# Strassen's seven-product block form for the products with x, in an inference step of a hybrid decoder

## The chip, the cores and the metric

The kernel runs on one core of a Trainium2 chip. The metric is the device time of one execution in microseconds (us). The core has a matrix engine (TensorE, PE in the profile; PEld is its weight load), three engines for elementwise work (VectorE or DVE, ScalarE or ACT, GpSimd or POOL) and SyncE (SP), from whose queue most DMAs are issued. The engines work side by side and wait for each other by semaphores. SBUF is the on-chip memory; PSUM, with banks of 512 fp32 columns, takes TensorE's results. GpSimd is not used on PSUM here.

## What is computed

One step of a decoder with two layers, fp32 in and out, for 1024 prompt tokens and 8 single new tokens (1032 tokens together, model width 1024):

```
# layer 0: gated short convolution          # layer 1: differential attention, 8 heads
b, c, h = split(x @ w_in, 3)                kv = x @ w_kv;  q = rope(x @ w_q)
y = (b * conv3(c * h)) @ w_out              y = rms_norm(softmax(q0 k0) v - lam * softmax(q1 k1) v) @ w_o
# both layers
x = layer_norm(alpha * x + y)
x = layer_norm(alpha * x + (silu(x @ w_gate) * (x @ w_up)) @ w_down)      # inner width 2816
```

The 8 new tokens attend to 256 cached positions each, gathered by a page table, and to themselves (below: decode). Outputs are x after layer 1, the new keys and values, and the last inputs of the convolution.

## The kernel before

All activations lie transposed: 128 features on the partitions, tokens along the columns. The tokens are cut into 3 chunks of 344 columns (CH). Every product has to be exact to nearly fp32, so both operands are split into two fp32r parts, a rounded one and the residual: x into xhf and xlf, a weight tile into whi and wlo. `dense` (L243) makes three matmuls for each of the K tiles: whi by the rounded x (L248), whi by the residual of x (L249), wlo by the rounded x (L251).

A weight tile is 128 x 1024 (8 K tiles by 128 outputs, or as many numbers in another cut). `Stream` (L101) loads it on SP's queue (L112), ACT rounds it to whi (L122) and POOL subtracts to get wlo (L123); 6 pairs are kept ahead. There are 196 such tiles: 24 for w_in, 8 for w_out, 8 each for Q, K, V and w_o, 88 for gate and up of both layers together, 44 for w_down. Where a pass covers one chunk alone, its tiles are loaded and split again for the next chunk.

The program is a list of blocks (L212), each with its weight tiles and its operations. Between the operations `Side` (L141) takes steps of generators that run beside: the layer norms, the first splits of x, the decode. `need` (L256) finishes the norm of a chunk before its first use. Tile, the framework, orders the instructions of each engine and adds the semaphores.

- `conv_mixer` (L423): for each of 8 feature tiles three products c, h, b and the convolution; then w_out, in two halves of K; the second half runs chunk by chunk.
- `ffn` (L384): groups of four (once two) inner tiles; gate and up for the three chunks, silu times up (L398), split into hh and hl (L262, L263), then the down products of the group, added to the residual stream (L359). The first group has its chunks in separate blocks, the last runs chunk by chunk.
- `layer_norm` (L266): sums of the chunk by a matmul with ones, subtraction, squares on ACT, their sum on DVE (L280), reciprocal root, scaling (L305), and the split of the normed x (L300, L302).
- Q and K (`qk_op`, L535) are written to DRAM in their parts. V (`v_steps`, L570) has x as the stationary operand, so that it comes out with tokens on the partitions: products of 128 tokens by 256 columns. Half of V (two of four pairs, EARLY, L184) is made with Q and K.
- `decode` (L617) runs beside K and V: gathers by POOL's queue (L653), products and sums on DVE (L675 to L732).
- `attention` (L770): per head and row block of 128 scores for two maps, exponentials, their difference, transposes, product with V. The other half of V fills it: pieces of `v_steps` are put between the score products. At its end the first products with w_o begin (`begin_project`, L960).
- `project` (L967), the feed-forward of layer 1, and `last_norm` (L318) for the last chunk.

```python
for k in range(nk):
    h, l = xs(k)
    T.matmul(ps, lhsT=hi[:, k, n0:n0 + nn], rhs=h, start=(k == 0), stop=False)
    T.matmul(ps, lhsT=hi[:, k, n0:n0 + nn], rhs=l, start=False, stop=False)
for k in range(nk):
    T.matmul(ps, lhsT=lo[:, k, n0:n0 + nn], rhs=xs(k)[0], start=False, stop=(k == nk - 1))
```

## Time and profile before

| | |
|---|---|
| Time, median of 3 runs | 2614.7 us (2613.64 to 2619.28) |
| The profiled execution | 2612.27 us, its span 2610.5 us |
| TensorE busy | 2495.7 us, 15818 matmuls |
| DVE, ACT, POOL busy | 1299.2, 846.8, 990.6 us |
| Mean granted TensorE clock | 0.982 |

The span goes from the first to the last instruction; little lies around it. Matmuls overlap in the profile (one is shown with some 325 ns, and yet one begins every 157 ns), so their price is read from how many begin in a stretch, not from the duration of one. The duration of an operation on DVE or POOL includes what it waits inside its engine. "x637" behind a busy time is the number of instructions.

### The profile page before, as it was taken

The numbers are of one execution on the slowest core, as the hardware profiler recorded it, in microseconds if no ns is written. First come the engines' busy times: TensorE is split into PE (matmuls) and PEld (weight loads), VectorE is DVE, ScalarE is ACT, GpSimd is POOL, SyncE is SP. The second block draws the span as 40 slices with busy tenths as digits, with TensorE's granted clock in tenths as the row PEclk, the third lists the DMA queues.
The fourth block names the chain that finished last, engine by engine and source line by source line (L and its number), as shares of the span: only waits on it lengthen the run. The fifth ranks groups of instructions, "written<-read, shape, count | busy, mean of one in ns | idle before, by whom it ended". The sixth has DMA issues, their size and how long they took to land. (4 is left out here: it accounts for less than half of the span.)

```text
span 2610.5 us, 38657 instructions
## 1 busy us (share of the span) xinstructions
PE 2495.7 (96%) x15818; PEld 2442.3 (94%) x15818; DVE 1299.2 (50%) x1980; ACT 846.8 (32%) x1534; POOL 990.6 (38%) x545
## 2 busy tenths in 40 slices
PE   8999989999999999989999999898999999999996
PEld 8999889999999999978997899798899999999995
DVE  6335897213222222788387477859723222222277
ACT  3213444211212121443332477734421111111243
POOL 5226555221212223545467243454541222212463
PEclk9999999999999999999999999999999999999998
DMA  4114333111111112336698667543321111111241
GB/s 166 49 49 138 107 116 111 65 41 49 49 49 49 49 42 77 116 127 227 192 328 304 189 181 207 156 164 104 113 97 41 49 49 49 41 48 51 89 152 67
DMA packets 109217, 283.72 MB, mean 109 GB/s; under 512 B 12872, under 2 KB 41960, under 8 KB 108144
## 3 DMA queue, kind: packets, MB, share of 16 engines
q1 hardware_dynamic: 101968, 254.28, 29.8%
q0 software_dynamic: 4608, 16.78, 1.7%
q10 hardware_dynamic: 2464, 10.20, 1.1%
q8 instruction: 124, 2.03, 0.3%
q14 instruction: 53, 0.43, 0.1%
HBM read 242.04 MB, written 39.17 MB: 108 GB/s over the span
## 5 line engine op out<-in xcount | busy, mean ns | idle before, releaser
L123 POOL TENSOR_TENSOR wlo<-wst,whi 128x1024 fp32r<-128x1024 f32 x336 | 832.6, 2484 | 1343.2 <-PE mm L251 662.7
L248 PE MATMUL mm<-xhf,whi 128*128 128x344 f32 x3264 | 1047.6, 325 | 15.7 <-DVE rb L359 7.8
L249 PE MATMUL mm<-xlf,whi 128*128 128x344 f32 x3264 | 1042.0, 323 | 1.8 <-DVE xlf L263 1.8
L248 PEld LDWEIGHTS mm<-xhf,whi 128*128 128x128 f32 x3264 | 622.2, 191 | 19.8 <-DVE rb L359 8.4
L249 PEld LDWEIGHTS mm<-xlf,whi 128*128 128x128 f32 x3264 | 621.7, 190 | 5.2 <-DVE xlf L263 2.5
L122 ACT CAST whi<-wst 128x1024 fp32r<-128x1024 f32 x336 | 351.8, 1049 | 838.3 <-PE mm L249 666.2
L251 PE MATMUL mm<-xhf,wlo 128*128 128x344 f32 x3264 | 587.6, 322 | 0.6 <-POOL wlo L123 0.6
L251 PEld LDWEIGHTS mm<-xhf,wlo 128*128 128x128 f32 x3264 | 533.0, 189 | 1.7 <-POOL wlo L123 0.9
L398 DVE TENSOR_TENSOR t<-mm,t 128x344 f32<-128x344 f32 x132 | 67.8, 514 | 570.4 <-PE mm L251 567.6
L249 PE MATMUL mm<-hl,whi 128*128 128x344 f32 x1056 | 335.3, 323 | 9.2 <-DVE hl L263 9.2
L248 PE MATMUL mm<-hh,whi 128*128 128x344 f32 x1056 | 331.0, 323 | 2.9 <-ACT hh L262 2.0
L251 PE MATMUL mm<-hh,wlo 128*128 128x344 f32 x1056 | 213.5, 320 | 0.0
L249 PEld LDWEIGHTS mm<-hl,whi 128*128 128x128 f32 x1056 | 199.5, 189 | 10.6 <-DVE hl L263 10.6
L248 PEld LDWEIGHTS mm<-hh,whi 128*128 128x128 f32 x1056 | 199.3, 190 | 4.2 <-ACT hh L262 2.6
L359 DVE TENSOR_TENSOR rf<-mm,rf 128x344 f32<-128x344 f32 x192 | 98.2, 514 | 181.4 <-PE mm L251 181.1
L359 DVE TENSOR_TENSOR rb<-mm,rb 128x344 f32<-128x344 f32 x168 | 86.2, 515 | 184.6 <-PE mm L251 184.5
L251 PEld LDWEIGHTS mm<-hh,wlo 128*128 128x128 f32 x1056 | 175.6, 188 | 0.0
L263 DVE TENSOR_TENSOR hl<-t,hh 128x344 fp32r<-128x344 f32 x132 | 144.4, 1096 | 62.0 <-ACT hh L262 61.7
L392 ACT ACTIVATE t<-mm 128x344 f32<-128x344 f32 x132 | 60.0, 457 | 284.3 <-PE mm L251 283.9
L262 ACT CAST hh<-t 128x344 fp32r<-128x344 f32 x132 | 62.9, 479 | 217.9 <-DVE t L398 217.8
L822 DVE CUSTOM_DVE_ANT_0 p<-S,mw 128x256 f32<-128x256 f32 (+7 forms) x128 | 94.4, 753 | 47.1 <-PE S L816 24.3
L824 ACT ACTIVATE p<-p,nm 128x256 f32<-128x256 f32 (+7 forms) x128 | 99.0, 774 | 34.0 <-DVE nm L822 33.5
(194 smaller groups left out, 2382.2 us busy)
## 6 DMA issues: line engine op xcount, KB each, us to landing
wst<-in_wts SPq DMA_DIRECT2D x336, 512.0 KB
qh<-qh SPq DMA_DIRECT2D x64, 128.0 KB
ql<-ql SPq DMA_DIRECT2D x64, 128.0 KB
rf<-in_xT SPq DMA_DIRECT2D x12, 344.0 KB
stash<-rf SPq DMA_DIRECT2D x3, 1376.0 KB
qh<-hi SPq DMA_DIRECT2D x24, 172.0 KB
ql<-lo SPq DMA_DIRECT2D x24, 172.0 KB
out_k<-t SPq DMA_DIRECT2D x24, 172.0 KB
```

Of the source, the lines that this page charges most:

```text
L122: self.nc.scalar.copy(out=hi, in_=st)
L123: self.nc.gpsimd.tensor_tensor(out=lo, in0=st, in1=hi.bitcast(F32), op=ALU.subtract)
L248: T.matmul(ps, lhsT=hi[:, k, n0:n0 + nn], rhs=h, start=(k == 0), stop=False)
L249: T.matmul(ps, lhsT=hi[:, k, n0:n0 + nn], rhs=l, start=False, stop=False)
L251: T.matmul(ps, lhsT=lo[:, k, n0:n0 + nn], rhs=xs(k)[0], start=False, stop=(k == nk - 1))
L262: A.copy(out=hi, in_=src)
L263: V.tensor_tensor(out=lo, in0=src, in1=hi.bitcast(F32), op=ALU.subtract)
L359: V.tensor_tensor(out=R[:, n], in0=ps, in1=R[:, n], op=ALU.add)
L392: A.activation(out=hid[f, c], in_=ps, func=AF.Silu)
L398: V.tensor_tensor(out=sg, in0=ps, in1=sg, op=ALU.mult)
L822: V.tensor_tensor_reduce(out=p[:, 0:n], in0=s[:, 0:n], in1=mw[:, SEQ - n:SEQ], scale=1.0, scalar=1e30, op0=ALU.add, op1=ALU.min, accum_out=nm)
L824: A.activation(out=p[:, 0:n], in_=p[:, 0:n], func=AF.Exp, bias=nm, scale=-1.0, accum_out=l)
```

## The change

The tokens are cut into two chunks of 516, each with half of the prompt and of the new tokens, and each chunk into two halves of 258 columns. A product of two weight tiles (256 outputs), 1024 inputs and 516 tokens is seen as 2 x 2 blocks: outputs by tile, K by halves of 512, tokens by halves of 258. Winograd's variant of Strassen's form makes the four output blocks from 7 block products instead of 8:

- `Stream._prepare` forms the seven weight operands of a pair of tiles: three blocks as they are and four sums, the sums on POOL; each is split by ACT and POOL. Weights now come as half tiles of 128 x 512 (raw, 5 buffers); 4 split operands are kept ahead.
- `blocks_of` and `sums_of` form the seven x operands of a chunk: B11, B21 and B22 as they are and four sums T1 to T4, the sums on POOL; all are split by ACT and DVE. They are made at the start and in every layer norm whose result is multiplied.
- `wino` makes the seven products, some of which add up in PSUM, and joins them on DVE; a `Sink` says what becomes of the four output blocks.

This form is used for w_in, Q, K, V, gate and up, the products with the normed x. The products with w_out, w_o and w_down stay in the old form (`exact`), with 258 columns. Feed-forward groups have two inner tiles (11 groups); the first and the last run chunk by chunk. V is made like K, with features on the partitions, transposed by TensorE and stored, all of it ahead of the attention. The attention has no filling any more; its Q and K tiles lie in the places of x, and its output goes straight to the operand of w_o. The stash of the residual stream moves: chunk 0 is stored before Q, and its place is used for the rotary table and for temporaries; decode has 3 buffers for gathers of K instead of 6. The convolution's result takes the place of x in SBUF, so that w_out's sum reads x from DRAM again. The last norm is no longer shared with POOL. The core of the diff:

```diff
+B11, B21, B22, T1, T2, T3, T4 = range(7)
+NS = 7
+
+WINO = [("A", B11, True), ("B", T2, True), ("A", B21, False), ("B", T3, False), ("C", T1, True), ("E", T4, True),
+        ("C", B22, False)]
...
+    def _prepare(self):
+        task = self.done
+        kind, base = self.tasks[task]
+        self._load(task)
+        nc, g = self.nc, self.nc.gpsimd
+
+        def total(a, b, op):
+            t = self.pool.tile([P, 512], F32, tag="ws", name="ws", bufs=self.sums)
+            g.tensor_tensor(out=t, in0=a, in1=b, op=op)
+            return t
+
+        if kind is None:
+            src = self.raw[base]
+        else:
+            a11, a21, a22, a12 = (self.raw[base + i] for i in range(4))
+            if kind == 1:
+                self.s[1] = total(a21, a22, ALU.add)
+                self.s[2] = total(self.s[1], a11, ALU.subtract)
+            elif kind == 3:
+                self.s[3] = total(a11, a21, ALU.subtract)
+            elif kind == 6:
+                self.s[4] = total(a12, self.s[2], ALU.subtract)
+            src = {0: a11, 2: a12, 5: a22, 1: self.s.get(2), 3: self.s.get(3), 4: self.s.get(1), 6: self.s.get(4)}[kind]
+        hi = self.pool.tile([P, 512], F32R, tag="whi", name="whi", bufs=self.ring)
+        lo = self.pool.tile([P, 512], F32R, tag="wlo", name="wlo", bufs=self.ring)
+        nc.scalar.copy(out=hi, in_=src)
+        g.tensor_tensor(out=lo, in0=src, in1=hi.bitcast(F32), op=ALU.subtract)
         self.ready.append((hi, lo))
-        self.split += 1
+        self.done += 1
...
+        while self.done < min(len(self.tasks), self.taken + self.ring):
...
-    WB, SB = 6, 3
-    RATE = 3
-    PIECES = 4
-    RATE0 = 8
+    RATE = 2
     LAG = 2
-    BEGIN = 4
...
+    xh = [xpool.tile([P, NS, KP, CH], F32R, name=f"xh{p}") for p in range(NP)]
+    xl = [xpool.tile([P, NS, KP, CH], F32R, name=f"xl{p}") for p in range(NP)]
+
+    zh, zl = ([x[p][:, T1:].rearrange("p s k n -> p (s k n)").rearrange("p (k n) -> p k n", k=KT) for p in range(NP)]
+              for x in (xh, xl))
     scr = {n: dram.tile([D, NTOK], F32, name=n) for n in ("qh", "ql", "kh", "kl")}
...
+    def exact(ps, terms, first=True, last=True, **kw):
+
+        for i, ((wh, _), (h, l)) in enumerate(terms):
+            T.matmul(ps, lhsT=wh, rhs=h, start=(first and i == 0), stop=False, **kw)
+            T.matmul(ps, lhsT=wh, rhs=l, start=False, stop=False, **kw)
+        for i, ((_, wl), (h, _)) in enumerate(terms):
+            T.matmul(ps, lhsT=wl, rhs=h, start=False, stop=(last and i == len(terms) - 1), **kw)
...
+    def wino(keys, ps, sink, rate=RATE):
+
+        def f():
+            sinks = {p: sink(p) for p in ps}
+            for p in ps:
+                need(p)
+            bank, m, u = {}, {}, {}
+            for i, (b, slot, begins) in enumerate(WINO):
+                w = ws.take()
+                if i == 3:
+                    while later:
+                        later.pop(0)()
+                for p in ps:
+                    if begins:
+                        bank[b, p] = mm()
+                    ps_ = bank[b, p]
+                    exact(ps_, [(cut(w, k), (xh[p][:, slot, k], xl[p][:, slot, k])) for k in range(KP)], begins,
+                          skip_group_check=not begins)
+                    s = sinks[p]
+                    if i == 0:
+                        m[p] = tmp()
+                        A.copy(out=m[p], in_=ps_)
+                    elif i == 1:
+                        u[p] = s.place("u")
+                        V.tensor_tensor(out=u[p], in0=ps_, in1=m[p], op=ALU.add)
+                    elif i == 2:
+                        s.c11(ps_)
+                    elif i == 3:
+                        V.tensor_tensor(out=m[p], in0=ps_, in1=m[p], op=ALU.add)
+                    elif i == 4:
+                        c = s.place("c22")
+                        V.tensor_tensor(out=c, in0=ps_, in1=m[p], op=ALU.add)
+                        s.c22(c)
+                    elif i == 5:
+                        c = s.place("c21")
+                        c = m[p] if c is None else c
+                        V.tensor_tensor(out=c, in0=ps_, in1=m[p], op=ALU.add)
+                        s.c21(c)
+                    else:
+                        V.tensor_tensor(out=u[p], in0=ps_, in1=u[p], op=ALU.add)
+                        s.c12(u[p])
+                    side.step(rate)
+        block([("wino", *keys)], f)
...
+    def blocks_of(p, q=None):
+        X = R[p]
+        for slot, k0, cs_ in ((B11, 0, 0), (B21, KP, 0), (B22, KP, 1)):
+            if q is None or q == cs_:
+                split_into(xh[p][:, slot], xl[p][:, slot], X[:, k0:k0 + KP, HALVES[cs_]])
+                yield
+
+    def sums_of(p):
+        X = R[p]
+        for j in range(KP):
+            b11, b12, b21, b22 = (X[:, k, HALVES[c]] for k in (j, KP + j) for c in range(2))
+            t = {}
+            for slot, a, b in ((T1, b12, b11), (T2, b22, None), (T3, b22, b12), (T4, b21, None)):
+                t[slot] = tmp()
+                G.tensor_tensor(out=t[slot], in0=a, in1=t[slot - 1] if slot in (T2,) else t[T2] if slot == T4 else b,
+                                op=ALU.subtract)
+                split_into(xh[p][:, slot, j], xl[p][:, slot, j], t[slot])
...
+            if not final:
+                yield from blocks_of(p, q)
...
+            yield from sums_of(p)
...
+    def project(kind, p, base, ln, begun=()):
+        for n in range(KT):
+            def f(n=n):
+                w = [ws.take(), ws.take()] if n >= len(begun) else None
+                b = base(n) if base is not None else None
+                for q, cols in enumerate(HALVES):
+                    if w is None:
+                        ps = begun[n][q]
+                    else:
+                        ps = mm()
+                        exact(ps, [(cut(w[k // KP], k % KP), (zh[p][:, k, cols], zl[p][:, k, cols])) for k in range(KT)])
+                    add_product(p, n, q, ps, True, ALPHA, None if b is None else b[:, cols])
+                    side.step(2 * RATE)
+                if n == KT - 1:
+                    norm(p, *ln)
+            block([("half", (kind, n))] if n >= len(begun) else [], f)
...
+            def put(self, a, b, q):
+                V.tensor_tensor(out=a, in0=a, in1=b, op=ALU.mult)
+                split_into(self.hh[:, HALVES[q]], self.hl[:, HALVES[q]], a)
...
+        last = NF // 2 - 1
+        for g in range(NF // 2):
+            for ps in ([[0], [1]] if g in (0, last) else [[0, 1]]):
+                for f in (2 * g, 2 * g + 1):
+                    up_and_gate(f, ps)
+                down(g, ps, (1, l, l == 1) if g == last else None)
...
+        for j in range(0, KT, 2):
+            for ps in ([[0], [1]] if j == 0 else [[0, 1]]):
+                for jj in (j, j + 1):
+                    wino((("in", "c", jj), ("in", "h", jj)), ps, lambda p, jj=jj: Carry(p, jj))
+                if j + 2 < KT:
+                    wino((("in", "b", j), ("in", "b", j + 1)), ps, lambda p, j=j: Mul(p, j))
...
+        for p in range(NP):
+            wino((("in", "b", KT - 2), ("in", "b", KT - 1)), [p], lambda p: Mul(p, KT - 2))
+            block([], lambda p=p: parts(p))
+        for p in range(NP):
+            project("mix", p, base(p), (0, 0))
...
+    produce("q", (2, 4, 6), [[0], [1]])
+    produce("q", (0,), [[0, 1]])
+    part_q = part()
+    produce("k", (2, 4, 6, 0), [[0, 1]])
+    produce("v", (0, 2, 4, 6), [[0, 1]])
...
-                if left and (2 * (t + 2) + half) % 3:
-                    with tc.issue_after(st_["pe"]) if "pe" in st_ else nullcontext():
-                        next(fill)
-                    left -= 1
-                    if not left:
-                        release()
```

## Rows read from the trace of the kernel before

**Rows 1.** the page, part 1: busy us (share) xinstructions of each engine
```profile
PE 2495.7 (96%) x15818; PEld 2442.3 (94%) x15818; DVE 1299.2 (50%) x1980; ACT 846.8 (32%) x1534; POOL 990.6 (38%) x545
```
**Rows 2.** windows: length, busy us (xinstructions) of PE PEld DVE ACT POOL, clock, DMA
```profile
0.00:100.00 100.00, 91.48 (x557) 90.23 (x558) 53.30 (x93) 33.75 (x60) 42.70 (x35) 1.00 0.34 124
300.00:400.00 100.00, 87.42 (x505) 84.57 (x504) 88.99 (x114) 36.78 (x55) 58.22 (x36) 0.93 0.34 112
600.00:700.00 100.00, 100.00 (x637) 100.00 (x636) 22.04 (x36) 20.24 (x32) 20.00 (x9) 1.00 0.13 43
1100.00:1200.00 100.00, 82.54 (x463) 79.38 (x462) 83.41 (x115) 40.42 (x60) 51.92 (x32) 0.91 0.43 149
1300.00:1500.00 200.00, 190.66 (x1299) 171.04 (x1298) 142.40 (x193) 73.97 (x161) 106.80 (x61) 0.99 0.81 271
2500.00:2610.00 110.00, 84.83 (x504) 80.72 (x502) 79.08 (x107) 49.16 (x80) 46.94 (x24) 0.88 0.29 102
```
**Rows 3.** one line's operations: ns min/median/max, first and last start, forms
```profile
L263 DVE TENSOR_TENSOR hl<-t,hh x132: 452/518/2282, 417.2 to 2573.0; 128x344 fp32r<-128x344 f32 x132
L359 DVE TENSOR_TENSOR rf<-mm,rf x192: 498/517/518, 151.5 to 1193.6; 128x344 f32<-128x344 f32 x192
L302 DVE TENSOR_SCALAR rf<-rf,prm_t x48: 378/385/2534, 300.0 to 1237.6; 128x344 f32<-128x344 f32 x48
L675 DVE TENSOR_TENSOR rf<-rf x16: 1207/1212/3422, 1319.4 to 1372.7; 128x1024 f32<-128x1024 f32 x16
L123 POOL TENSOR_TENSOR wlo<-wst,whi x336: 2339/2402/6677, 5.8 to 2566.8; 128x1024 fp32r<-128x1024 f32 x168
```
**Rows 4.** timeline, DVE and POOL: start us, us together, operation, count
```profile
301.98 6.22 DVE L302 TENSOR_SCALAR rf<-rf,prm_t 128x344 f32<-128x344 f32 x6
302.06 5.01 POOL L123 TENSOR_TENSOR wlo<-wst,whi 128x1024 fp32r<-128x1024 f32 x2
```
**Rows 5.** timeline, TensorE, same columns
```profile
1394.83 1.11 PE L580 MATMUL vps<-whi,xhf 128*128 128x256 f32 x8
1395.78 1.10 PE L580 MATMUL vps<-whi,xlf 128*128 128x256 f32 x8
```
**Rows 6.** groups of POOL: count, busy us, mean ns, idle before, releasers
```profile
L123 POOL TENSOR_TENSOR wlo<-wst,whi 128x1024 fp32r<-128x1024 f32 x336 | 832.6, 2484 | 1343.2 <-PE mm L251 662.7 <-ACT whi L122 652.6 <-issue 8.3
L653 POOL DMA_INDIRECT rf<-in_cache_v,idx x16 | 27.0, 1688 | 7.4 <-DMA wst<-in_wts 4.2 <-issue 2.8 <-DVE rf L675 0.3
L653 POOL DMA_INDIRECT rf<-in_cache_k,idx x16 | 18.3, 1142 | 15.8 <-DVE sc L677 8.2 <-DMA rf<-qrow_d 2.7 <-DVE idx L622 2.3
L836 POOL TENSOR_TENSOR p<-p,p 128x640 f32<-128x640 f32 x8 | 12.5, 1558 | 0.6
L836 POOL TENSOR_TENSOR p<-p,p 128x384 f32<-128x384 f32 x8 | 8.1, 1017 | 0.6
```
**Rows 7.** groups of TensorE, same columns
```profile
L248 PE MATMUL mm<-xhf,whi 128*128 128x344 f32 x3264 | 1047.6, 325 | 15.7 <-DVE rb L359 7.8 <-ACT xhf L262 6.2 <-ACT t L392 0.9
L248 PE MATMUL mm<-hh,whi 128*128 128x344 f32 x1056 | 331.0, 323 | 2.9 <-ACT hh L262 2.0 <-DVE t L398 0.8
L248 PE MATMUL mm<-gh,whi 128*128 128x344 f32 x192 | 60.9, 330 | 6.8 <-ACT gh L262 6.8
L580 PE MATMUL vps<-whi,xhf 128*128 128x256 f32 (+1 forms) x288 | 42.8, 286 | 0.0
```
**Rows 8.** windows of five heads and of one; last row: tile vps alone
```profile
1488.90:1644.60 155.70, 148.50 (x1135) 140.46 (x1134) 114.76 (x294) 115.49 (x328) 62.30 (x66) 0.99 0.70 200
1644.60:1669.40 24.80, 23.79 (x164) 21.13 (x163) 21.35 (x59) 21.40 (x62) 10.85 (x13) 0.97 0.86 222
1488.90:1644.60 155.70, 48.42 (x314) 39.99 (x312) 5.08 (x14) 0.99 0.70 200
```
**Rows 9.** window near the start, columns as in rows 2
```profile
10.00:15.00 5.00, 5.00 (x20) 4.43 (x19) 5.00 (x16) 2.57 (x5) 3.39 (x1) 1.00 1.03 413
```
**Rows 10.** group of ACT, columns as in rows 6
```profile
L262 ACT CAST hh<-t 128x344 fp32r<-128x344 f32 x132 | 62.9, 479 | 217.9 <-DVE t L398 217.8
```

More of the change, by code (lines that the diff above doesn't have):

```diff
@@ L20 @@
 KT = D // P
+KP = KT // 2
 SEQ = 1024
@@ L29 @@
 DFF = 2816
+NF = DFF // P
 PAST = 256
@@ new lines, in _load @@
+    def _load(self, task):
+        need = self.tasks[task][1] + (4 if self.tasks[task][0] is not None else 1)
+        while len(self.raw) < len(self.loads):
+            i = len(self.raw)
+            if sum(self.last[j] >= task for j in range(max(0, i - 16), i)) >= self.raws:
+                assert i >= need
+                return
+            t = self.pool.tile([P, 512], F32, tag="raw", name="raw", bufs=self.raws)
+            u, h = self.loads[i]
+            self.nc.sync.dma_start(out=t, in_=self.wts[u, h])
+            self.raw[i] = t
@@ L360, in add_product @@
+    def add_product(p, n, q, ps, total, scale=None, base=None):
+        r = R[p][:, n, HALVES[q]]
+        if scale is not None:
+            V.scalar_tensor_tensor(out=r, in0=r if base is None else base, scalar=scale, in1=ps, op0=ALU.mult, op1=ALU.add)
+        else:
+            V.tensor_tensor(out=r, in0=ps, in1=r, op=ALU.add)
         if total and n:
             if n == 1:
-                while sums:
-                    side.drain(lnq[next(iter(sums))])
-                sums[c] = pools["s"].tile([P, CH], F32, tag="sum", name="sum", bufs=1)
@@ L365, in add_product @@
-            V.tensor_tensor(out=sums[c], in0=R[:, 0] if n == 1 else sums[c], in1=R[:, n], op=ALU.add)
-    def consume(uids, per, zs, nk, chunks, ln=None, first=0):
-        def op(c, i, q):
-            return lambda w: add_product(c, i * per + q, w[0], zs(c), nk, q * P, ln is not None)
-        def norm(c):
-            def f(w):
-                lnq[c] = side.add(last_norm(c, ln[1]) if c == NCH - 1 and ln[-1] is True else layer_norm(c, *ln))
-            return f
-        for i, u in list(enumerate(uids))[first:]:
-            ops = [(nk // 4 if nk > 3 else 1, op(c, i, q)) for q in range(per) for c in chunks]
-            if ln is not None and i == len(uids) - 1:
-                ops += [(0, norm(c)) for c in chunks]
-            block([u], ops)
+                sums[p, q] = pools["s"].tile([P, CH], F32, tag="s", name="sum")
@@ L599, in decode_setup, with produce @@
+    def produce(which, order, passes):
+        for ps in passes:
+            for t in order:
+                wino(((which, t), (which, t + 1)), ps, lambda p, t=t: Keep(p, which, t))
     def decode_setup():
         dp = pools["d"]
-        dec["rope"] = dp.tile([P, 2, NTOK], F32, name="rope_t")
-        A.dma_start(out=dec["rope"], in_=rope)
         dec["cst"] = dp.tile([P, 35], F32, name="dcst_t")
```

866 lines of the change are left out of this document (396 added, 470 removed).

## The prediction

> **What bounds the kernel now.** I read four views in this order. The page gives TensorE 96% of the span, POOL 38% and DVE 50% [rows 1]. The windows of 100 us show why: in a middle window of a feed-forward layer 637 matmuls of 344 columns run, one every 0.157 us, without idle time; POOL is busy 20% there, DVE 22% [rows 2]. So products set the time, except in some stretches. With 0.157 us as the price of a matmul, a window of n such matmuls loses its length less 0.157n: 12.5 us in the first, 20.7 from 300, 27.3 from 1100, 30.9 in the last [rows 2]; ten such windows lose 139.2. With the idle 9.3 us of 1300 to 1500, where other shapes run [rows 2], that is 149 us. These stretches are the start, the changes from one sub-layer to the next (layer norm) and the stage of Q, K, V and decode.
>
> The third view, durations of one line, says what holds them up. hl<-t,hh, an fp32 operation on DVE with two tensors in SBUF, takes 0.518 us as a rule and up to 2.28. rf<-mm,rf, as wide but with one tensor in PSUM, never exceeds 0.518 [rows 3]. The timeline shows the cause: six tensor_scalar operations on DVE, usually 0.385 each [rows 3], take 6.22 us together where two weight subtractions on POOL take 5.01 [rows 4]. While POOL works on SBUF, such a DVE operation waits for POOL's to end. I call these two loads together the port. POOL and DVE are half idle on average, but not in the lossy windows: DVE 83 to 89 of 100 us, POOL 52 to 58 [rows 2].
>
> **Prices.** A matmul of 256 columns comes every 0.118 us (eight from 1394.83 to 1395.78) [rows 5]; with the step to 0.157 at 344, 258 columns cost 0.119. No row has 258; 344 scaled by columns gives 0.118, so the bounds are narrow. POOL's fp32 add takes 1.017 us for 384 and 1.558 for 640 columns [rows 6]: 1.29 for 512 and, along the same line, 0.75 for 258. DVE with two tensors in SBUF takes 0.52 for 344 and 1.21 for 1024 [rows 3]: 0.43 for 258, 0.69 for 516, 1.22 for 1032.
>
> **1. Products.** Before: 4512 matmuls each on L248, L249 and L251, 13536 in all [rows 7], 2125 us; and 864 of V (288 on each of three operand pairs, [rows 7]), 102 us: 2227. After: 136 weight tiles (24 of the mixer, 24 of Q, K, V, 88 of gate and up) make 68 pairs, each 7 products x 2 token chunks x 4 K tiles x 3 parts = 168 matmuls; the 60 others (mixer out, w_o, down) take 96 each. 11424 + 5760 = 17184 x 0.119 = 2041 us. Gain 186.
>
> **2. V out of the attention.** 384 V matmuls (45 us) filled the attention. Five heads with 314 of them took 155.7 us, one without took 24.8 [rows 8]. Without filling five heads take 124: 31.7 saved, not 45, since DVE and ACT are busy 21 of those 24.8 us. Cost against item 1: +14.
>
> **3. Weight preparation.** Before, a tile is one POOL subtraction of 2.40 us [rows 3]. After, a pair of tiles needs four sums and seven residuals of 512 columns, 11 x 1.29 = 14.2 us, anew for every pass. A pass over both chunks covers this with 19.9 us of matmuls, a pass over one with 10.0. The code makes 83 such preparations, and 84 of 2.6 us for the other tiles; with the x sums below POOL carries some 1490 us instead of 832.6 [rows 6]. The ring holds four tasks ahead, about 8 us of POOL's work, so POOL can't save up for a bad stretch.
>
> **4. x blocks.** Every layer norm now also forms T1 to T4: 16 POOL subtractions of 258 (12.0 us) and 16 splits; the norm's DVE work on two SBUF tensors is 14 x 0.43 + 4 x 1.22 + 3 x 1.22 + 16 x 0.43 = 21.5 us per chunk. The running sums add 14 x 0.43 = 6.0 to each pass that ends in a norm.
>
> **5. The stretches, anew.** For each: TensorE; POOL; DVE on two SBUF tensors; then the loss against TensorE if POOL alone counts, and if all of DVE's time is added.
> - Start and first three pairs, one chunk after the other: 60; 6 x 14.2 + 24 = 109, and 5 until x is there; 33: 54 to 87. x comes fast (413 GB/s, [rows 9]), POOL is the limit.
> - Last mixer pair: 20; 28 less 8 stored; 14: 0 to 14.
> - Second half of an output projection, with the norm of chunk 0 (twice): 46; 33; 28: 0 to 29 in all.
> - First feed-forward group, chunk 0, with the norm of chunk 1 (twice): 31; 46; 25: 28 to 78. Chunk 1 (twice): 31; 34; 3: 4 to 12.
> - Last group, chunk 0 (twice): 0 to 8. Chunk 1 with the norm of chunk 0: 31; 46; 31: 14 to 45; in layer 1, without x sums: 2 to 22.
> - Q in passes of one chunk: 30; 55; 26, then 30; 43; 4: 38 to 68.
> - Last Q pair, K, V and decode: 193; POOL 9 x 14.2 + 45 of gathers (16 x 1.69 and 16 x 1.14, [rows 6]) + 5 = 178; DVE 76, of which decode 40 x 1.21: 0 to 61.
>
> Bottom 140, top 424. In the timeline row six operations of 2.31 us added 1.21 to POOL's 5.01, 52% of their time [rows 4]; I take that share: 140 + 0.52 x 284 = 288.
>
> By the Trainium skill (Advanced Engine Details and Errata, Mode Summary) GpSimd and two-port vector instructions block each other; by that sentence alone an fp32 add of two tensors would run beside POOL and the sum would be near the bottom. The row of hl, an add of two tensors, disagrees [rows 3], so the measured share stands.
>
> **6. Small terms.** A down product starts right behind its last gate/up product, and its second operand then passes DVE (0.43), ACT, DVE, ACT, DVE; ACT's cast takes 0.479 for 344 [rows 10]. That is about 2.5 to 3.5 us, and the order of the four tiles hides only 0.7 to 2: 0 to 6 us, I take 2.5, in each of 18 middle groups: 45 (0 to 108). 64 transposes of V, 128 columns each, at no more than the 0.118 us of 256: 8. The last norm stays behind the last product: 28 (28 to 33). The first scores wait for K and Q loads into x slots that V's last product still reads: 5 (0 to 10).
>
> **Sum** against the profiled execution, 2612.3 us (span 2610.5; median of the runs 2614.7): 2612 - 186 + 14 - 149 = 2291 if no stretch lost anything. Plus 288 + 45 + 8 + 28 + 5 = 2665. Bottom: 2291 + 140 + 8 + 28 = 2467; top: 2291 + 424 + 108 + 8 + 33 + 10 = 2874. **Forecast 2665 us, slower by 2%.**
>
> **Rivals.** (a) DVE's work hides in POOL's own pauses (POOL waits for ACT's cast before each residual of a fresh sum) and the down chains hide behind other tiles: only POOL's own time counts, 2467 to 2600, about 2530. For it: TensorE keeps 100% in 600 to 700, and there every cast and subtraction is hidden [rows 2]. Against it: the 6.22 us of [rows 4]. It decides below the point where small terms and losses exceed 321: with the small terms as taken, if DVE's share is under 0.33. The sentence of the Trainium skill on two-port instructions, above, would give this case. (b) The preparation is worse than its sum: POOL waits for ACT's cast of each of three fresh sums per pair, some 0.6 to 0.8 us each, about 2.4 us, nowhere filled; some 30 one-chunk preparations lose 75 us more, and the passes over both chunks (14.2 + 2.4 + 3.4 of DVE against 19.9) start to lose too: 2740 to 2800. For it: POOL's idle time before wlo is mostly ended by ACT's whi, 652.6 us [rows 6]. Against it: the casts can be issued ahead where the raw tile is there. (c) It doesn't do what it says: 258 columns cost as much as 2227 / 17184 = 0.130 us, and the gain is gone. The 256-column rows [rows 5], with as many weight loads as matmuls [rows 1], nearly exclude this; it would give 186 more than the forecast, some 2850.
>
> **Numbers.** Forecast 0.46 (2600 to 2735), (a) 0.30, (b) 0.21, (c) 0.03. 8 in 10 lie between 2480 and 2800: below lies the fast end of (a), above the worst of (b) and (c). About 0.2% (5 us) is what a measurement of this kernel can tell from no change; the border at 2612 lies between (a) and the forecast. Faster 0.29, same 0.04, slower 0.67.
>
> **What would show it.** Item 1: 17184 matmuls of 258, one every 0.119 us in the middle groups. Item 2: heads of 25 us. Items 3 to 5: POOL near 1500 us and dense in the first 130 us, at the norms and in Q, with DVE's two-tensor operations at two or three times 0.43; TensorE idle there, its idle ended by POOL's residuals or by DVE's splits. Item 6: short waits for hl at each down product. The forecast is wrong if TensorE stays above 95% through the norms (then (a)), or if it also idles in the middle groups (then (b)).

## The result and the profile after

The changed kernel takes 2821.6 us (median, 2819.2 to 2822.4) where the kernel before takes 2615.4: 1.0785 times as long, with a 95% interval of 1.0766 to 1.0803. That is slower, as forecast, but by 206 us instead of 50, and 22 us above the top of the range. The profiled execution spans 2820.2 us.

The page, part 1, of the changed kernel (columns as in [rows 1]):

```profile
span 2820.2 us, 48587 instructions
PE 2447.8 (87%) x18690; PEld 2341.7 (83%) x18690; DVE 1771.3 (63%) x3070; ACT 1065.7 (38%) x2312; POOL 1715.7 (61%) x1397
```

TensorE falls from 96% of its span to 87%, POOL rises from 990.6 us [rows 1] to 1715.7. Windows of the changed kernel (columns as in [rows 2]): a mixer stretch, the start, the first feed-forward group, a stretch of middle groups, the Q passes of one chunk, the middle of the V stage, the first two heads and five later ones.

```profile
200.00:300.00 100.00, 100.00 (x832) 100.00 (x832) 57.88 (x96) 31.95 (x60) 76.80 (x74) 1.00 0.18 53
0.00:134.00 134.00, 82.03 (x507) 75.09 (x508) 93.58 (x129) 50.08 (x97) 122.69 (x115) 0.91 0.28 95
428.00:546.00 118.00, 82.56 (x536) 75.05 (x535) 91.03 (x129) 67.38 (x138) 98.57 (x85) 0.80 0.17 51
600.00:700.00 100.00, 98.87 (x818) 98.26 (x817) 50.09 (x103) 27.78 (x58) 52.33 (x41) 1.00 0.15 43
1231.00:1362.00 131.00, 82.32 (x515) 74.17 (x515) 101.03 (x131) 68.90 (x143) 118.35 (x106) 0.76 0.43 140
1540.00:1590.00 50.00, 25.77 (x69) 7.32 (x69) 30.07 (x27) 3.23 (x7) 18.38 (x14) 0.76 0.44 147
1641.00:1704.00 63.00, 47.08 (x300) 39.89 (x298) 45.06 (x115) 40.72 (x111) 19.54 (x21) 0.84 0.55 165
1704.00:1839.00 135.00, 119.88 (x824) 103.03 (x823) 115.68 (x298) 105.42 (x312) 56.11 (x60) 1.00 0.53 137
```

Where TensorE is fed it runs 832 matmuls in 100 us, one every 0.1202 us. In the first group it runs only 536 in 118 us, in the Q passes 515 in 131; POOL is busy 84 and 90% of these, DVE 77%. 17184 products at 0.1202 are 2065 us; the other 755 are losses and the attention. The table cuts the trace at the first product of each stage and gives each stage's length less 0.1202 per product, for the changed kernel and for five of the runs below; the first column is what the prediction took, with its ends.

```
us lost, by stage            forecast        after  no weight  no x   no sums,  all prep.  last
                                                    sums       sums   no resid. on DVE     version
start, first pairs            71 (54-87)      73     47         73     32        43         41
last mixer pair                7 (0-14)       11      6          5      0         3          3
projections, second half      15 (0-29)       18     11         18      3         3         20
first groups, both layers     62 (32-90)     115     99         65     30       118         89
last groups, both layers      47 (16-75)      61     43         60     31        45         38
Q                             54 (38-68)      72     54         50     12        59         53
K, V, decode (*)              52 (20-81)      96     72         97     63        85         55
18 middle groups              45 (0-108)      35     19         36     17        33         32
attention                                    236    237        230    232       233        227
after the last product        28              31     31         31     31        31         24
the rest                                       6      5          8      5         5          5
(*) includes 20 us of decode's own TensorE work and of V's transposes, in the forecast too
```

### The profile page after: what moved, and what is told of

Same layout as the page of the kernel before. It is cut to its first block, busy times and chain, and to the rows that moved or that the text cites. A ratio compares the mean times of both kernels' runs of the same rounds, so it can differ in the third digit from the quotient of the medians.

```text
span 2820.2 us, 48587 instructions
## 1 busy us (share of the span) xinstructions
PE 2447.8 (87%) x18690; PEld 2341.7 (83%) x18690; DVE 1771.3 (63%) x3070; ACT 1065.7 (38%) x2312; POOL 1715.7 (61%) x1397
## 5 line engine op out<-in xcount | busy, mean ns | idle before, releaser
L291 PE MATMUL mm<-xh,whi 128*128 128x258 f32 x4320 | 1127.8, 293 | 143.0 <-ACT xh L284 45.1
L292 PE MATMUL mm<-xl,whi 128*128 128x258 f32 x4320 | 1118.9, 290 | 52.9 <-DVE xl L285 50.5
L291 PEld LDWEIGHTS mm<-xh,whi 128*128 128x128 f32 x4320 | 844.2, 196 | 166.8 <-ACT xh L284 51.2
L292 PEld LDWEIGHTS mm<-xl,whi 128*128 128x128 f32 x4320 | 843.8, 195 | 64.0 <-DVE xl L285 63.7
L168 POOL TENSOR_TENSOR wlo<-raw,whi 128x512 fp32r<-128x512 f32 x417 | 567.1, 1365 | 440.8 <-ACT whi L167 290.9
L294 PE MATMUL mm<-xh,wlo 128*128 128x258 f32 x4320 | 693.4, 289 | 7.9 <-POOL wlo L168 7.9
L168 POOL TENSOR_TENSOR wlo<-ws,whi 128x512 fp32r<-128x512 f32 x332 | 448.3, 1353 | 366.6 <-ACT whi L167 333.4
L294 PEld LDWEIGHTS mm<-xh,wlo 128*128 128x128 f32 x4320 | 601.5, 194 | 10.7 <-POOL wlo L168 10.1
L291 PE MATMUL mm<-hh,whi 128*128 128x258 f32 x1408 | 367.7, 290 | 34.0 <-DVE t L338 7.5
L292 PE MATMUL mm<-hl,whi 128*128 128x258 f32 x1408 | 377.0, 287 | 13.2 <-DVE hl L285 12.9
```

Source lines behind the costliest of these rows:

```text
L168: g.tensor_tensor(out=lo, in0=src, in1=hi.bitcast(F32), op=ALU.subtract)
L291: T.matmul(ps, lhsT=wh, rhs=h, start=(first and i == 0), stop=False, **kw)
L292: T.matmul(ps, lhsT=wh, rhs=l, start=False, stop=False, **kw)
L294: T.matmul(ps, lhsT=wl, rhs=h, start=False, stop=(last and i == len(terms) - 1), **kw)
```

## The experiments

Theories. P: while POOL works on SBUF, an operation of DVE on two SBUF tensors waits for it and the other way round, so the two loads add up. A: POOL's own time alone counts. D: DVE's queue as a whole is full. L: the norm's chain of dependent steps. Runs of one version lie up to 16 us apart (the kernel before, 2605.8 to 2621.8) and most versions ran once, so differences of the whole time under 10 us are not used, and small ones above it only with the stages that show them. The losses of the stages repeat better: those of the changed kernel and of the first run below, whose time did not change, agree within 2 us.

**What V's stage waits for.** From 1540 to 1590 TensorE runs little but decode's matmuls L857 (timeline of the changed kernel, TensorE: start, length, operation, count, idle before and what ended it):

```profile
1546.01 5.35 PE L857 MATMUL st<-rf,sel 128*8 128x512 f32 x8 [5.79 <-DVE rf L855]
1556.97 5.00 PE L857 MATMUL st<-rf,sel 128*8 128x512 f32 x8 [5.60 <-DVE rf L855]
1568.78 5.92 PE L857 MATMUL st<-rf,sel 128*8 128x512 f32 x8 [6.81 <-DVE rf L855]
1580.65 5.11 PE L857 MATMUL st<-rf,sel 128*8 128x512 f32 x8 [5.96 <-DVE rf L855]
1585.69 1.39 PE L663 MATMUL st<-cs,o 128*128 128x128 f32 x8
```

First I let decode's loop give up its turn more often:

```diff
             V.tensor_tensor(out=t, in0=t, in1=at[:, pg, b]..., op=ALU.mult)
-            yield
+            yield "op"
...
+                yield "op"
```

> One edit to the changed kernel (2821.6 us): decode's loop over the cached values gives up its turn more often, so that its 16 pairs of small matmuls are issued over the whole V stage instead of within its first half. In the changed kernel TensorE ran only these for some 46 us (about 1540 to 1586), waiting for the gathers. Theory 1 (TensorE works in program order, and the products of V stand behind matmuls whose gathered values come late): with the matmuls spread the products of V fill the waits, 35 to 46 us gained, 2776 to 2787 us, the V stage about 105 instead of 149.5 us. Rival (the port to SBUF is what is full there: gathers, multiplications and weight preparation need this time in any order): TensorE waits elsewhere for the same time, 2810 to 2825 us.

Measured 2819.5 us, no change, but the edit didn't reach its aim: the 32 matmuls still stand in one row in TensorE's program. The last row above says why: V's transposes L663 write a statistics bank (st), and there are two, both held by decode's accumulators. So the second edit gives the transposes another bank:

```diff
-            tp = stat()
+            tp = mm(512)
             for j in range(4):
                 T.transpose(tp[:, j * P:(j + 1) * P], src[...], ident)
```

> One edit to the changed kernel (2821.6 us): the transposes of V take their PSUM bank from the six of the products instead of the two of the statistics. In the changed kernel decode holds both statistics banks as accumulators from its first to its last gathered page, so a transpose of V, which comes next in program order and needs one of them, can only stand behind all 32 of decode's small matmuls, and the products of V behind it. Theory 1 (it is this order that made TensorE wait some 46 us for gathers at 1540 to 1586): the 32 matmuls spread between the products, 35 to 46 us gained, 2776 to 2787 us. Rival (gathers, their multiplications and the weight preparation fill DVE and POOL in any order): most of it given back, 2800 to 2820 us.

Measured 2806.3 us. The matmuls are spread, and V's stage lost 15 us less. The same window now holds 255 matmuls instead of 69, and TensorE waits 0.5 us for L855 instead of 24.2 (windows, then waits of TensorE from 1488 to 1650: what waits for what, us, times, longest):

```profile
1540.00:1590.00 50.00, 43.21 (x255) 33.00 (x254) 32.68 (x38) 9.82 (x21) 33.67 (x25) 0.90 0.60 195
1590.00:1641.00 51.00, 39.64 (x283) 33.14 (x282) 25.50 (x34) 14.87 (x27) 19.32 (x15) 0.89 0.81 249
...
PE mm L291 <- DVE o L323: 4.9, 2, 4.5
PE mm L291 <- ACT o L691: 4.8, 1, 4.8
PE st L886 <- DVE dec_o L881: 4.5, 1, 4.5
...
PE st L857 <- DVE rf L855: 0.5, 2, 0.3
```

So the order was real and cost 15 us: between the two expectations, nearer to the rival. The 46 us were more than could be had, since 21 of them are the time of the 32 matmuls themselves (the four rows above), which TensorE needs in any order; only 24.2 us were waits. That some 10 of these came back because POOL's and DVE's work, done before beside a waiting TensorE, now met the products (POOL 33.7 us of the first window instead of 18.4) is my reading.

**Sums of weights on DVE.**

```diff
-            g.tensor_tensor(out=t, in0=a, in1=b, op=op)
+            nc.vector.tensor_tensor(out=t, in0=a, in1=b, op=op)
```

> One edit to the changed kernel (2821.6 us): the four sums of weights per pair are made on DVE (by estimate 0.69 us each) instead of POOL (1.29 to 1.42 each); POOL is left with 9.0 us per pair. Theory P (in the stretches where one chunk is worked at a time, POOL's time and DVE's time on two SBUF tensors add up): each of the 30 one-chunk preparations gains 4 x 0.6 to 0.7 = 2.4 to 2.9 us, 70 to 85 in all, 2735 to 2755 us. Rival A (POOL's own time alone counts): 5.2 to 5.7 us for each of the 30, 155 to 170 gained, 2650 to 2670. Rival L (the stretches wait for a chain of dependent steps: norm, cast, residual): nothing gained, or up to 40 lost since DVE is the busier engine there, 2815 to 2860.

Measured 2793.4 us, 28 less. A falls: 155 us were to come. P's 70 to 85 are missed as well; the start gains 16, Q 6, but the first groups lose 5 and the middle groups 9, as D would have it.

**No sums of weights.** They are left out, and plain blocks stand in their place.

```diff
-            if kind == 1:
-                self.s[1] = total(a21, a22, ALU.add)
...
-            src = {0: a11, 2: a12, 5: a22, 1: self.s.get(2), 3: self.s.get(3), 4: self.s.get(1), 6: self.s.get(4)}[kind]
+            src = {0: a11, 2: a12, 5: a22, 1: a21, 3: a22, 4: a21, 6: a12}[kind]
```

> The changed kernel with the four sums of weights per pair left out: the seven products of a pair use the plain blocks as operands, so that only casts and residuals remain to be made for them. This prices the sums. Theory P and rival A alike: 5.2 to 5.7 us of POOL for each of the 30 one-chunk preparations, and the wait for the cast of a fresh sum falls away: 155 to 230 gained, 2590 to 2665 us. Rival L (chain of the norm, not the amount of preparation): under 50 gained, 2770 us or more.

Measured 2691.1 us: 130 less, under the 155 of P and A and over L's 50. The sums cost 26 us at the start, 18 in Q, 24 in K and V, 17 in the middle groups, but only 16 in the first groups, where the losses are largest.

**No x sums in the norms.**

```diff
-                    exact(ps_, [(cut(w, k), (xh[p][:, slot, k], xl[p][:, slot, k])) for k in range(KP)], ...
+                    exact(ps_, [(cut(w, k), (xh[p][:, slot % 3, k], xl[p][:, slot % 3, k])) for k in range(KP)], ...
...
-        if not final:
-            yield from sums_of(p)
```

> The changed kernel with T1 to T4 left out of the layer norms (16 subtractions on POOL, 16 casts on ACT and 16 residuals on DVE per chunk and norm); the products that read them read the plain blocks B11, B21, B22 instead. The first x blocks, before the mixer, are made as before. This prices item 4. Theory D (in the stretches with a norm DVE and the first product's wait for T1 to T4 set the time, not the preparation of weights): the three norms lose 20 to 35 us less each, 2720 to 2765 us. Rival P (POOL's preparation of weights is what they wait for): only POOL's 12 us per chunk go, partly hidden, 2770 to 2800 us.

Measured 2740.4 us: 81 less, 50 of it in the first groups and 22 in Q. As theory D had it; the sums, casts and residuals of T1 to T4 are what those stages wait for first. In the changed kernel they show as waits of TensorE in the first groups of layer 0 and, below, of layer 1; every one of these waits ends with a part of T1 to T4:

```profile
PE mm L291 <- ACT xh L284: 11.1, 7, 3.5
PE mm L292 <- DVE xl L285: 10.6, 6, 4.2
...
PE mm L292 <- DVE xl L285: 15.0, 6, 5.3
...
PE mm L291 <- ACT xh L284: 3.4, 1, 3.4
```

**Neither sums of weights nor x sums.** Both edits above.

> Both sets of sums left out: the four sums of weights per pair and T1 to T4 of the norms (each alone gave 131 and 81 us). Theory 1 (they lie in different stretches, or one behind the other): the gains add, 2600 to 2620 us. Theory 2 (they load the same queues beside each other, and either alone had already brought the next limit to the front): the gains overlap, 2630 to 2670 us. Theory 3 (below some load DVE and POOL no longer hinder each other): more than the sum, under 2595 us.

Measured 2604.9 us: 217 less, for 130 and 81 alone. The gains add. If its sums cost nothing, the block form would be about level with the kernel before.

**No residuals of weights either.** POOL then prepares nothing; the third matmul of a product reads the cast weights again.

```diff
-        g.tensor_tensor(out=lo, in0=src, in1=hi.bitcast(F32), op=ALU.subtract)
-        self.ready.append((hi, lo))
+        self.ready.append((hi, hi))
```

> Both sets of sums and all residuals of weights left out (the third matmul of each product uses the cast weights again), so that POOL prepares nothing and ACT only casts: what is left is the norms, the x blocks, decode and the attention. Without the sums alone it was 2604.9 us. Theory P (the seven residuals, 9 us for 10 us of products in a one-chunk pass, still hold the start, Q and K): 50 to 80 us less, 2525 to 2555 us. Rival (what is left waits for the norms' own chain, decode and the attention): under 25 less, 2580 us or more.

Measured 2522.0 us: 83 less again, a little over P's 50 to 80. Without all three, Q loses 12 us instead of 72, the first groups 30 instead of 115. So L by itself falls: the norm's own steps are still there, and the stages around them hardly wait once T1 to T4 and POOL's preparation are gone. The page of this run:

```profile
span 2520.2 us, 46183 instructions
PE 2356.8 (94%) x18690; PEld 2287.9 (91%) x18690; DVE 1325.9 (53%) x2974; ACT 1028.0 (41%) x2216; POOL 168.3 (7%) x220
```

**All weight preparation on DVE.** The sums as above, and

```diff
-        g.tensor_tensor(out=lo, in0=src, in1=hi.bitcast(F32), op=ALU.subtract)
+        nc.vector.tensor_tensor(out=lo, in0=src, in1=hi.bitcast(F32), op=ALU.subtract)
```

> The changed kernel with all weight preparation (four sums and seven residuals per pair, and the residuals of the other tiles) on DVE instead of POOL; POOL keeps the x sums, the gathers and a few small operations. Per pair 11 x 0.69 = 7.6 us of DVE by estimate, instead of 14.2 of POOL. Theory P (the two loads add up because one waits for the other, so the quicker engine should do it all): the sum of both falls by 6.6 us per one-chunk preparation, up to 200 gained, if DVE's other work (3.4 us per pair and chunk with SBUF, as much again with PSUM, and 21.5 us of each norm) leaves room: 2640 to 2760 us. Rival L or DVE full: 2800 us or more, the middle groups also idle, since DVE's orders stand in line behind adds that wait for TensorE.

Measured 2725.7 us: 96 less, in P's range, although DVE was busy 77% of the first group and of Q already and carries it all now. One line's operations (count, ns min/median/max), first of the changed kernel, then of this run:

```profile
L285 DVE TENSOR_TENSOR hl<-t,hh x176: 407/953/1532, 463.9 to 2776.6; 128x258 fp32r<-128x258 f32 x176
L327 DVE TENSOR_TENSOR t<-mm,t x136: 408/427/430, 48.7 to 2765.5; 128x258 f32<-128x258 f32 x136
L168 POOL TENSOR_TENSOR wlo<-ws,whi x332: 1252/1292/2360, 11.9 to 2762.7; 128x512 fp32r<-128x512 f32 x166
```

```profile
L285 DVE TENSOR_TENSOR hl<-t,hh x176: 412/419/429, 423.6 to 2678.8; 128x258 fp32r<-128x258 f32 x176
L168 DVE TENSOR_TENSOR wlo<-ws,whi x332: 622/683/1618, 9.3 to 2661.1; 128x512 fp32r<-128x512 f32 x166
```

This is theory P's mechanism by itself. With POOL preparing weights, a subtraction of two SBUF tensors on DVE takes 0.95 us at the median and up to 1.53; without, it never takes over 0.43. The trace of the changed kernel shows it alone, too: of these 176 subtractions 113 overlap an operation of POOL and have a median of 1.23, the 63 others one of 0.43 with none above. An operation as wide with one operand in PSUM takes 0.43 beside POOL or not. And POOL suffers too: of its 1081 preparing operations the 504 with no DVE operation on two SBUF tensors beside them take at most 1.32 us, the 577 others up to 2.36. DVE needs 0.68 for what takes POOL 1.29.

**First groups over both chunks.**

```diff
-            for ps in ([[0], [1]] if g in (0, last) else [[0, 1]]):
+            for ps in ([[0], [1]] if g == last else [[0, 1]]):
```

> The changed kernel (2821.6 us) with the first feed-forward group of each layer worked in passes over both chunks instead of one chunk after the other: four of the 30 one-chunk preparations fall away, but TensorE has nothing to do while the norm of chunk 1 runs. Theory P (the amount of preparation sets these stretches): of the 116 us lost there 30 to 50 are gained, 2770 to 2790 us. Rival D (the norm with its x blocks, some 45 us of DVE's time, sets them, and the pass over chunk 0 hid some of it): the norm of chunk 1 lies open, nothing gained to 30 lost, 2820 to 2850 us.

Measured 2818.5 us: no difference that counts, as D rather than P had it. The first groups lose 107 for 115: what four preparations fewer save is mostly given back, by D because the norm of chunk 1 lies open.

**V ahead of the attention, in the kernel before.** Here line 184 and the call ahead of the attention's loop:

```diff
-    EARLY = 2
+    EARLY = 4
...
+        release()
```

> The kernel before (2615.4 us) with one edit: all four quarters of V are made ahead of the attention instead of two; nothing of the block form is in it. This measures item 2 alone. By the five heads of 155.7 us with 314 V matmuls and the one of 24.8 without: 14 us slower, some 2629 us. By the heads of the changed kernel, 27.0 us each without filling (five in 135 instead of 124): 25 us slower, some 2640. If the V matmuls were filling time in which TensorE had nothing else at hand, all their 45 us come on top: 2660.

Measured 2636.9 us, 1.0085 times the kernel before (1.0068 to 1.0103): 22 us, 18 to 27. Item 2 had 14. In this run, too, a head without filling takes 27 to 28 us, from the second head on.

**Squares summed on TensorE.**

```diff
-                if n:
-                    V.tensor_tensor(out=ssq, in0=was if n == 1 else ssq, in1=sq, op=ALU.add)
+                T.matmul(var, lhsT=ones, rhs=sq, start=(n == 0), stop=(n == KT - 1))
```

> One edit to the changed kernel (2821.6 us): the eight squares of a norm's variance are summed by eight matmuls on the ones matrix (TensorE, idle in these stretches) instead of seven additions on DVE (0.42 to 1.0 us each there) and one matmul. Theory D (in a stretch with a norm DVE's queue is full, so what leaves it comes off the stretch): 14 additions, 6 to 10 us, per chunk and norm; in the six that lie open some 25 to 50 us gained, 2770 to 2797 us. Rival (the chain of dependent steps or POOL sets them): within 10 us of 2821; slower if products stand behind matmuls that wait for squares.

Measured 2805.2 us: 16 less, between the rival's 10 and D's 25 to 50. The first groups gain 7, the last stretch 6.

**Combinations.** The preparation on DVE with V's transposes in the products' banks:

> All weight preparation on DVE and V's transposes in the banks of the products (each alone gave 96 and 15 us). If they add: 2705 to 2715 us. Rival (in the V stage DVE, which now carries the preparation as well as decode, has no room for the second): 2718 to 2730 us.

Measured 2704.9 us: they add. With both sums of the norm on TensorE:

> As the run with all weight preparation on DVE and V's transposes in the banks of the products, and both sums of a norm (the running sums of x and those of the squares) are formed by matmuls on the ones matrix instead of DVE's additions. Theory D (DVE's queue is full in the stretches with a norm, most of all with the preparation on it): 28 additions of 0.42 us per chunk and norm leave it, 40 to 80 us under the kernel without this, 2630 to 2670 us. Rival (chain): 2690 to 2715 us.

Measured 2682.9 us, 22 less: between the theories. The first groups lose 79 instead of 118, but the second halves of the projections 34 instead of 3. With the squares alone there:

> Preparation on DVE, V's transposes in the banks of the products, and of the norm's sums only the squares on TensorE (the running sums of x again by DVE's additions). The kernel with both on TensorE (2682.9 us) lost 14.0 and 19.9 us in the second halves of the output projections, where 1.5 and 1.8 were lost before. If the running sums did this (their eight matmuls wait for the last tile of the projection): 25 us gained, 2655 to 2662 us. Rival (they were also what helped the first groups, where 18 and 18 us came off): 2680 to 2700 us.

Measured 2666.0 us, 17 less than with both; but only 8 of them in the projections, which still lose 26 us where 3 were lost without the squares. So it is mostly the squares that wait there. With DVE doing all the preparation, the squares bring the first groups from 118 to 79 us; with POOL doing it they brought 7. So in the first groups, and only with the preparation on DVE, DVE's queue is the limit, as D has it. Part of it is the clock: with the squares on TensorE the granted clock in layer 0's first group is 0.90 instead of 0.78, which by the products at the lower clock explains some 6 of the 39 us. The next run sets P against D for the rest: the four sums go back to POOL.

> The same kernel with the four sums of weights per pair on POOL again and the seven residuals on DVE. Theory P (POOL's time and DVE's on two SBUF tensors add up, so the quicker engine should do all): 2.4 us more for each of the 30 one-chunk preparations, some 40 to 70 us slower than with all of it on DVE. Theory D (DVE's queue as a whole is the limit in the stretches with a norm and in Q, K, V): it is relieved of 2.8 us per pair, 20 to 60 us faster. Within 15 us of it: the two balance.

Measured 2719.3 us, 53 more, as P expects and against D: start +10, first groups +22, middle groups +14, Q +7; only K, V and decode gain 9. Q in passes over both chunks:

> The kernel with preparation on DVE, V's transposes in the products' banks and the squares on TensorE, and the first three pairs of Q in passes over both chunks: three preparations fewer (3 x 7.6 us of DVE), but the norm of chunk 1 lies open. If the amount of preparation sets Q: 10 to 25 us less than without this edit. If the norm's chain sets it: within 10 us, or slower.

Measured 2670.8 us, no difference that counts, as expected if something other than the amount of preparation sets Q there. The x sums on DVE as well, with the preparation on DVE:

```diff
-                G.tensor_tensor(out=t[slot], in0=a, in1=...
+                V.tensor_tensor(out=t[slot], in0=a, in1=...
```

> The kernel with preparation on DVE, V's transposes in the banks of the products and the squares on TensorE (2666.0 us), and the x sums T1 to T4 on DVE too (by estimate 0.43 us each instead of 0.75 on POOL). Theory P (POOL's and DVE's time on two SBUF tensors add up): 16 x 0.32 = 5.1 us for each of eight chunks, 20 to 40 us in all, 2626 to 2646 us. Rival D (in the stretches with a norm DVE's queue as a whole is the limit by now): 0 to 30 us slower, 2666 to 2695 us. Neither is below the kernel before (2614 us).

Measured 2659.8 us (2654.1 to 2666.9), no difference that counts from the 2666.0 without it. It is 1.018 times the kernel before (1.015 to 1.0211): the best of the versions that compute everything, and still slower than the kernel before. The same edit alone, with the preparation on POOL:

> One edit to the changed kernel (2821.6 us): T1 to T4 of the norms and of the first x blocks are formed on DVE instead of POOL, where the weight preparation stays. Theory P: as above, 20 to 40 us, and more where the first product waited for T1 to T4 behind weight preparation in POOL's queue, 2765 to 2800 us. Rival D: DVE is the busier engine at the norms, 2820 to 2850 us.

Measured 2810.7 us, 11 less. Both lie between P and D: which engine forms the x sums matters little, though having them costs 81.

## Why the prediction was right and wrong

**Right:** the sign, the counts and where the time goes. 17184 products, the losses at the start, the norms and Q, little in the middle groups, and DVE's splits first among TensorE's waits. Waits of TensorE over the whole changed kernel:

```profile
PE mm L292 <- DVE xl L285: 50.5, 26, 5.3
PE mm L291 <- ACT xh L284: 45.1, 16, 13.4
PE st L396 <- DVE ssq L392: 32.4, 10, 9.5
PE mm L291 <- ACT whi L167: 26.5, 25, 4.0
PE st L857 <- DVE rf L855: 24.2, 4, 6.8
...
PE mm L292 <- DVE hl L285: 12.9, 18, 5.6
```

**Item 5 is the step that failed: one share of DVE's time for all stretches, and no term for what the first product of a chunk waits for.** I took 0.52 of DVE's time from one burst of six operations beside two of POOL [rows 4]. The stages lost 426 us (table, less the 20 of decode and transposes) where 288 was taken and 424 was the top, the case in which all of DVE's time adds to POOL's. The start came as forecast (73 for 71). Q shows the sum best: 98 us of POOL and 30 of DVE make 128, and the passes took 131. The first groups had 108 per layer by the same sum (46 + 34 and 25 + 3) and took 118 and 124, more than the top; so did K, V and decode. The last groups lost 61, between the 47 taken and the 75 of the top. So the share was not one number: from 0.6 at the start to about 1 in Q.

That the whole sum comes near the total doesn't show that single loads cost their length. Without the weight sums 5.2 us of POOL fall away in each preparation, 31 us in Q and 41 in the first groups, and these gained 18 and 16. Without T1 to T4, 19 us per chunk by item 4, the two first groups, with a norm of chunk 1 in each, gained 50, and Q, with one, 22. The waits shown with that run say why: T1 to T4 stand at the end of a chunk's norm, and its first products wait for them one after the other, 40 us in the first groups and 26 in Q. Item 5 priced loads and had nothing for this row of steps.

Why one burst misled: in it DVE had operations at hand for every pause of POOL; that in the stages each waits in turn for the other's results is how I read it, it was not tested by itself. The lengthened operations of both engines are shown above; POOL's preparation and x sums came to some 1593 us for the 1490 of item 3. Some 59 of the 426 us are products at the lower clock (last section), for which I had no term either; how much of them would have been waiting in any case is open.

**Also in item 5, decode:** the forecast took 32 us for the last Q pair, K, V and decode, beside TensorE's own work; it lost some 76. 15 of these are the two statistics banks that decode holds while V's transposes want one, a resource for which I had no term. Some 43, these 15 probably among them, remain in the run without T1 to T4 and without any preparation on POOL, so most of this loss isn't the preparation's; what the rest is stays open. The loads before the first scores (item 6) were waited for 5.1 us, for the 5 taken, but the first two heads took 63.0 us where two later ones take 54: TensorE also waits 6.4 us there for decode's last step.

**Item 1:** 0.1202 us per product instead of 0.119, +24 us in all; 4 of these are a slip, since 17184 x 0.119 is 2045 and not 2041.

**Item 2** was mis-sized: 22 us for 14 in the run with the kernel before. One head without filling [rows 8] read 24.8; five of the changed kernel read 135.0 / 5 = 27.0. And the 31.7 us saved were read for 314 V matmuls and set against all 384.

**Item 4** left out DVE's work that doesn't meet POOL. In the first group's first pass the reciprocals alone take 3.5 us (groups of DVE, changed kernel, 428 to 498; columns as in [rows 6]), and the splits and sums of squares stand at 1.8 to 2 times the 0.43 taken:

```profile
L285 DVE TENSOR_TENSOR xl<-t,xh 128x258 fp32r<-128x258 f32 x16 | 13.9, 883 | 2.9 <-ACT xh L284 2.9
L392 DVE TENSOR_TENSOR ssq<-ssq,t 128x258 f32<-128x258 f32 x12 | 9.1, 755 | 0.4
L400 DVE RECIPROCAL rstd<-rstd 128x258 f32<-128x258 f32 x2 | 3.5, 1768 | 3.1 <-ACT rstd L399 3.1
```

**Item 6:** 35 us for 45, and only half of it as forecast. In layer 0 the 17.6 us of the nine middle groups do lie at the down products, but they fell to 0.6 when the weight sums were left out: the chain to hh and hl costs something only while POOL's sums lengthen its steps. In layer 1 the 17.8 us lie at other products, most of all at one that waits for a join on DVE (L323, 4.7 us in nine waits) and one that waits for a weight's cast (1.8), and 17.9 remained without the sums; why layer 1 differs is open. Waits for hl were 12.9 us in all. The end behind the last product took 31 for 28.

Together: +138 (item 5), +24 (item 1), -10 (down chains), +3 (end) and +1 for the rest, the attention among it, whose parts missed both ways: 156 of the 157 us between the forecast and this execution.

**The rivals.** (a) is excluded: POOL's time alone gives 140, not 426. (b) named the size best (2740 to 2800), but not for its reason: POOL hardly stands waiting for casts in Q, it is busy 118 of 131 us, where item 5 had 98 for its work. (c) is excluded by 832 matmuls in 100 us.

## What to carry to other kernels

Before work is moved from TensorE to POOL and DVE, count both engines' time on SBUF tensors stage by stage and reckon with the whole sum, not with a share read from one burst. Add what the first product of a stage waits for in a row, here T1 to T4 of its own chunk. Here the products saved 160 us, and all of POOL's preparation and the norms' x sums together cost 300. If both must work, let the quicker one do all of such work (96 us here; giving back a third of it to POOL cost 53). And look for what a moved step shares besides engines: two PSUM banks held by one loop put 32 waiting matmuls ahead of the products.

## What the runs showed of the hardware

**POOL and DVE hold each other up, both ways.** A subtraction of two SBUF tensors of 258 columns on DVE takes 0.43 us where no operation of POOL overlaps it and 1.23 at the median where one does; POOL's of 512 columns takes 1.29, and up to 2.36 beside such operations of DVE. With one operand in PSUM, DVE's takes 0.43 either way. The Trainium skill (SBUF — State Buffer, SBUF: two separate sides) says that a DVE operation with two SBUF inputs and a GpSimd operation that reads SBUF exclude each other: the one that starts first holds the pair of ports that they share for its whole length, and the other waits. The lengths with and without overlap and the unaffected PSUM form agree with it.

**TensorE's clock costs where it has waited.** The granted clock was 1.00 from 200 to 300, where TensorE never stood idle, and 0.76 in the Q passes, where it waited over a third of the time. Of the 17184 products 685 came 0.217 us after the one before instead of 0.120. I count these as run at the lower of the clock's two levels, 1.2 instead of 2.4 GHz: 475 of them begin where the trace has that level granted, and of the 16121 that came at the quick pace only 7 do. They cost 66 us, part of the losses above. In the kernel before, 180 came 0.287 after instead of 0.158, 23 us; the lower clock stood in its rows already (0.93, 0.91, 0.88 in [rows 2]), and I had made no term of it.
